# Row maxima of a neighbourhood attention: one head a product over 128 rows, or two heads in two 64-row halves

## The chip, the cores and the metric

One Trainium2 chip, one of its cores. The metric is the device time of one execution of the whole program, in microseconds (us). The engines of a core are TensorE (PE in the profile, its weight loads PEld), VectorE (DVE), ScalarE (ACT), GpSimd (POOL) and SyncE (SP, here only an issuer of DMAs). Each takes its instructions in a fixed order; they wait for each other by semaphores.

## What is computed

Two layers of a diffusion backbone over 2048 latent tokens, 256 context tokens and 1024 channels. Layer 0 mixes latent attention and gated linear attention. Layer 1, which the change is about, is a neighbourhood attention of 16 heads of 64 channels: the tokens lie on a grid of 32 rows by 64 columns, and each query sees the keys in a window of 8 by 16 around it, with a bias from a table, and all 256 context tokens.

```python
def odd_mixer(h, hc, w_in, q_gain, k_gain, rpb, w_out, update_ctx):
    q, k, v, z = ...                       # h @ w_in, split in four; q and k normed per head
    o = neighborhood_attention(q_x, k_x, v_x, k_c, v_c, rpb)
    y = jnp.dot(o.reshape(...) * jax.nn.silu(z_x), w_out)

# in neighborhood_attention, per grid row:
    s_lat = jnp.einsum('bqhd,brkhd->bhqrk', qr, kb) * scale + bias
    s_lat = jnp.where(col_mask, s_lat, -jnp.inf)
    s_ctx = jnp.einsum('bqhd,bchd->bhqc', qr, k_ctx) * scale
    p = jax.nn.softmax(jnp.concatenate([s_lat, s_ctx], axis=-1), axis=-1)
    o = p[..., :kr * GRID_W] @ vb + p[..., kr * GRID_W:] @ v_ctx
```

The softmax needs, for every query and head, a number near the maximum of its scores to subtract before the exponential. The kernel computes these maxima (the "maxima" below) ahead of the attention proper.

## The kernel before

The program runs in stages. Layer 0 comes first, then `odd_qk` projects q and k of layer 1, then `odd_vz` projects v and z and computes the maxima beside it, then `odd_attention` and the output projection follow. The change is in `odd_vz` and in the helper `weave`.

**The projections in `odd_vz`.** There are 18 tiles of 128 tokens (2 of context, 16 latent) and four column blocks of 512, `j` = 4, 5 for v and 6, 7 for z. A cell is one (tile, block); 66 of the 72 are computed here. A cell is 8 steps of `mm3_steps` (L129 to L131), each of three 128-row products into one PSUM bank called "gm", of which there are two. A v cell ends with a copy by ScalarE into `ovz` and two stores on GpSimd's DMA queue (L1201). A z cell ends with a tanh by ScalarE, an operation by VectorE (L1227), four transposes into a bank "tp" (L1230), a copy `ozt` by ScalarE and a store. When a tile is finished, the next one's activations are loaded into `x` and split in `reload` (L357 is its VectorE part).

**The maxima in `maxes`.** The loop runs over 16 heads. Two heads, a pair, share the key tile `mk` (128 rows: 64 channels of either head). Each head loads a bias table `mtab` (L1248, 899 KB) into one of two buffers, and GpSimd adds the row mask and the column mask to it (L1249, L1250). Then come 16 blocks `R` of 128 queries (8 grid rows by 16 columns; `g` is the row group, `c` the column group). Every fourth block, 512 queries are loaded into `mq` (L1258) and copied by ScalarE into the head's own 64 rows of a tile `mz` whose other 64 rows are zero, so that a product over all 128 rows of the array gives the scores of one head. Each block is two products: against the 256 context keys (L1264), two blocks to a bank, and against the window of keys (L1271), 264 to 480 columns, in a bank of its own. VectorE takes the context maxima of two blocks at once (L1266), and then goes through the window in 1 to 4 rectangular pieces, each adding a part of the table and taking the maximum (L1277, an operation and a read of its accumulator). The banks "mx" are five. After the 16 blocks the maxima are reduced (L1282), transposed (L1284), copied by ScalarE (`mr`) and stored in four DMAs on GpSimd's queue (L1288).

**The order.** `weave` alternates two generators: `main` gives the projections' steps, `side` those of the maxima, `ratio` of the second for one of the first. `issue_after(x)` keeps what is made inside it behind the instruction `x`. With a lag of 15, a projection step is only held behind the maxima's step that lies 15 back; within that, a scheduler decides where an instruction stands on its engine. It also decides, for the DMA queues of SP and POOL, in which order the loads and stores are issued. In this stage it spreads the products of the maxima singly between those of the projections.

Of the kernel before, what the change touches and what calls it, by code (L numbers as in the profile page):

```python
# [21 lines left out]
CTX = 256  # L22
T = SEQ + CTX
# [65 lines left out]
class Kern:  # L89
# [1113 lines left out]
    def odd_vz(self, ws, win, hT):  # L1203
        nc = self.nc
        self.z1 = self.scr("z1", (KD, P, SEQ), F32)
        self.M1 = self.scr("M1", (16, SEQ), F32)
        NR, NC = (len(b) for b in BLOCKS["q"])
        with ExitStack() as es:
# [6 lines left out]
            def cell(t, j):  # L1215
# [9 lines left out]
                    return  # L1225
                self.last_tanh = self.act(n[:], ps[:], AF.Tanh, scale=0.5)
                nc.vector.scalar_tensor_tensor(out=n[:], in0=n[:], scalar=1.0, in1=ps[:], op0=ALU.add, op1=ALU.mult)  # L1227
                pt = self.tl(pp, [P, 4, P], "tp", bufs=1)
                for i in range(4):
                    nc.tensor.transpose(pt[:, i, :], n[:, i * P : i * P + P], self.ident[:])  # L1230
                z = self.tl(sp, [P, 4, P], "ozt", bufs=1)
                self.act(z[:], pt[:])
                o = (t - NCT) * P
                nc.scalar.dma_start(self.z1[(j - 6) * 4 : (j - 6) * 4 + 4, :, o : o + P].rearrange("j p t -> p j t"), z[:])

            zq = [[self.tl(mp, [P, 512], f"mz{i}{a}", F32R, bufs=1) for a in range(2)] for i in range(2)]
            for i in range(2):
                for z in zq[i]:
                    nc.vector.memset(z[64 - i * 64 : 128 - i * 64].bitcast(F32), 0.0)

            def maxes():
                for h in range(16):
                    j, b = h // 2, (h % 2) * 64
                    if b == 0:
                        k = self.tl(mp, [P, T], "mk", F32R, bufs=2)
                        nc.sync.dma_start(k[:].bitcast(F32), self.K1[j])
                    tb = self.tl(mp, [P, NR, NC], "mtab", bufs=2)
                    nc.sync.dma_start(tb[:], self.i["rpb_q"][h].rearrange("p (r c) -> p r c", r=NR))  # L1248
                    nc.gpsimd.tensor_tensor(out=tb[:], in0=tb[:], in1=mk[:, :NR].unsqueeze(2).to_broadcast([P, NR, NC]), op=ALU.add)  # L1249
                    nc.gpsimd.tensor_tensor(out=tb[:], in0=tb[:], in1=mk[:, NR:].unsqueeze(1).to_broadcast([P, NR, NC]), op=ALU.add)  # L1250
                    m = self.tl(mp, [P, 16, 5], "mm")
                    nc.vector.memset(m[:], -3e38)
                    kl = k[:, CTX:].rearrange("d (r c) -> d r c", r=32)
                    for R in range(16):
                        g, c = divmod(R, 4)
                        if c == 0:
                            q = self.tl(mp, [P, 512], "mq", F32R, bufs=1)
                            nc.sync.dma_start(q[b : b + 64].bitcast(F32), self.Q1[0, j, b : b + 64, g * 512 : g * 512 + 512])  # L1258
                            zt = zq[h % 2][g % 2]
                            self.by_tile(zt[b : b + 64], q[b : b + 64])  # L1260
                        lh = zt[:, c * P : c * P + P]
                        if c % 2 == 0:
                            pc = self.tl(pp, [P, 2, CTX], "mx", bufs=5)
                        nc.tensor.matmul(pc[:, c % 2, :], lh, k[:, :CTX], start=True, stop=True)  # L1264
                        if c % 2 == 1:
                            nc.vector.tensor_reduce(out=m[:, R - 1 : R + 1, 0], in_=pc[:], axis=AX.X, op=ALU.max)  # L1266
                        (r0, nr), (c0, w) = rect("q", g, c)
                        ps = self.tl(pp, [P, 512], "mx", bufs=5)
                        a, n, d = even(c0, w)
                        ps = ps[:, : nr * n].rearrange("p (r c) -> p r c", r=nr)  # L1270
                        mm = nc.tensor.matmul(ps, lh, kl[:, r0 : r0 + nr, a : a + n], start=True, stop=True)  # L1271
                        ps = ps[:, :, d : d + w]
                        n = 1
                        for ro, ri, rn in pieces("q", 0, g, r0, nr):
                            for co, ci, cn in pieces("q", 1, c, c0, w):
                                s = ps[:, ro : ro + rn, co : co + cn]
                                nc.vector.tensor_tensor_reduce(out=s, in0=s, in1=tb[:, ri : ri + rn, ci : ci + cn], scale=1.0,  # L1277
                                                               scalar=-3e38, op0=ALU.add, op1=ALU.max, accum_out=m[:, R, n : n + 1])
                                n += 1
                        yield mm  # L1280
                    mc = self.tl(mp, [P, 16], "mc", bufs=1)
                    nc.vector.tensor_reduce(out=mc[:], in_=m[:], axis=AX.X, op=ALU.max)  # L1282
                    pt = self.tl(pp, [P, 512], "mx", bufs=5)
                    nc.tensor.transpose(pt[:16, :P], mc[:], self.ident[:])  # L1284
                    r = self.tl(mp, [P, P], "mr", F32R, bufs=1)
                    self.act(r[:16], pt[:16, :P], AF.Copy, scale=-1.0)
                    for g in range(4):
                        nc.gpsimd.dma_start(self.M1[h, g * 512 : g * 512 + 512].rearrange("(a c b) -> c a b", a=8, c=4),  # L1288
                                            r[4 * g : 4 * g + 4].rearrange("c (a b) -> c a b", a=8).bitcast(F32))
# [393 lines left out]
```

## Time and profile before

| | |
|---|---|
| Time, median of 3 runs | 3739.16 us (3738.85 to 3740.12) |
| The profiled execution's own time | 3741.73 us |
| Its span | 3739.6 us |
| `odd_vz` beside the maxima | about 2642 to 3071 us of the span |
| Projections alone after the last product of the maxima | to about 3104 us |
| GpSimd in 2642 to 3071 us | busy 178.1 of 429 us |

The page of the profile gives for each engine its busy time; groups of instructions by line give a count, the busy time, the mean of one, and the idle time ahead of them with what ended it. The busy time of a PE instruction contains pipelining: one projection product shows about 0.39 us while the next begins 0.23 us later. What a product costs the stage is therefore read from the starts of the instructions in the timeline, not from their durations.

### The profile page before, as it was taken

The numbers are of one execution on the slowest core, as the hardware profiler recorded it, in microseconds if no ns is written. First come the engines' busy times: TensorE is split into PE (matmuls) and PEld (weight loads), VectorE is DVE, ScalarE is ACT, GpSimd is POOL, SyncE is SP. The second block draws the span as 40 slices with busy tenths as digits, with TensorE's granted clock in tenths as the row PEclk, the third lists the DMA queues.
The fourth block names the chain that finished last, engine by engine and source line by source line (L and its number), as shares of the span: only waits on it lengthen the run. The fifth ranks groups of instructions, "written<-read, shape, count | busy, mean of one in ns | idle before, by whom it ended". The sixth has DMA issues, their size and how long they took to land.

```text
span 3739.6 us, 51736 instructions
## 1 busy us (share of the span) xinstructions
PE 3583.3 (96%) x18404; PEld 2768.3 (74%) x18404; DVE 2379.7 (64%) x4860; ACT 1437.7 (38%) x2741; POOL 1207.2 (32%) x1334
## 2 busy tenths in 40 slices
PE   8999989999999999999999999999899998898889
PEld 6988988888886666655657878887788885555567
DVE  4677656888866666697654344545678774666722
ACT  4445541111125555545552134444322223454400
POOL 1434330001011222212202233333344435776643
PEclk9999999999999999999999999999999998999899
DMA  7455462222252241434515545546544448777464
GB/s 254 137 165 160 128 172 94 84 75 86 74 137 66 69 114 56 115 88 137 142 51 169 165 148 149 146 142 182 183 141 143 130 116 223 186 182 201 141 194 132
DMA packets 365267, 512.18 MB, mean 137 GB/s; under 512 B 25825, under 2 KB 244913, under 8 KB 359106
## 3 DMA queue, kind: packets, MB, share of 16 engines
q1 hardware_dynamic: 322642, 425.49, 39.7%
q0 software_dynamic: 19712, 55.40, 4.9%
q10 hardware_dynamic: 22656, 27.99, 2.1%
q8 instruction: 146, 2.39, 0.3%
q14 instruction: 111, 0.91, 0.1%
HBM read 329.38 MB, written 179.37 MB: 136 GB/s over the span
## 4 chain that ended last, share of the span: by engine, by line
PE 79%; DVE 7%; DMA 6%; POOL 3%; ACT 3%; issue 2%; SPq 0%; POOLq 0%; DVEq 0%; ACTq 0%
PE gm L129 9%; PE gm L130 9%; PE gm L131 9%; PE av L905 7%; PE st L963 4%; PE mx L651 4%; PE st L964 3%; PE st L965 3%; PE pj L129 3%; PE pj L131 3%; PE pj L130 3%; DMA wraw<-w_od 2%; PE o L1393 2%; PE st L1363 2%; PE o L1375 1%
## 5 line engine op out<-in xcount | busy, mean ns | idle before, releaser
L954 DVE TENSOR_TENSOR acc<-acc,apt 128x512 f32<-128x512 f32 x512 | 364.5, 736 | 156.6 <-ACT apt L106 153.6
L106 ACT ACTIVATE apt<-st 128x512 f32<-128x512 f32 (+1 forms) x592 | 343.9, 593 | 283.9 <-PE st L965 246.5
L652 DVE TENSOR_REDUCE mm<-mx 128x1 f32<-128x512 f32 (+1 forms) x656 | 389.1, 628 | 82.2 <-PE mx L651 75.2
L905 PE MATMUL av<-apt,av 128*64 128x512 f32 (+1 forms) x1184 | 286.2, 597 | 0.0
L963 PE MATMUL st<-aq,akh 97*128 97x512 f32 (+1 forms) x592 | 254.1, 429 | 5.9 <-ACT apt L106 3.0
L1399 POOL TENSOR_TENSOR oacc<-oacc,opt 128x576 f32<-128x576 f32 (+6 forms) x192 | 221.4, 1179 | 86.6 <-ACT opt L106 84.9
L651 PE MATMUL mx<-mk,mq 96*128 96x512 f32 (+1 forms) x656 | 236.8, 373 | 5.8 <-DMA mq<-QT 4.6
L964 PE MATMUL st<-aq,akh 96*128 96x512 f32 (+1 forms) x592 | 235.1, 397 | 0.0
L965 PE MATMUL st<-aq,akl 96*128 96x512 f32 (+1 forms) x592 | 233.9, 396 | 0.0
L1277 DVE CUSTOM_DVE_ANT_1 mx<-mx,mtab 128x225 f32<-128x225 f32 (+13 forms) x576 | 183.6, 339 | 57.8 <-PE mx L1271 42.6
L106 ACT ACTIVATE u<-gm 128x352 f32<-128x352 f32 (+1 forms) x140 | 68.5, 497 | 369.5 <-PE gm L131 208.8
L905 PEld LDWEIGHTS av<-apt,av 128*64 128x64 f32 x1184 | 81.6, 137 | 155.4 <-issue 154.1
L1521 DVE TENSOR_TENSOR opt<-st,tab 128x64 f32<-128x64 f32 (+10 forms) x576 | 142.4, 315 | 79.9 <-PE st L1364 52.7
L963 PEld LDWEIGHTS st<-aq,akh 97*128 97x128 f32 x592 | 112.4, 190 | 99.0 <-issue 43.7
L1073 POOL TENSOR_TENSOR px<-py,px 128x512 f32<-128x512 f32 x64 | 86.3, 1349 | 234.3 <-DVE py L1072 223.0
L106 ACT ACTIVATE opt<-opt 128x930 f32<-128x930 f32 (+8 forms) x130 | 104.4, 805 | 138.9 <-DVE opt L1521 130.1
L1363 PE MATMUL st<-q,kt 128*128 128x480 f32 (+5 forms) x256 | 104.3, 409 | 47.7 <-DVE opt L1521 43.4
L651 PEld LDWEIGHTS mx<-mk,mq 96*128 96x128 f32 x656 | 121.7, 189 | 17.3 <-issue 5.0
L106 ACT ACTIVATE prh<-pr 128x1024 fp32r<-128x1024 f32 x32 | 33.8, 1057 | 261.6 <-PE pj L130 234.0
L965 PEld LDWEIGHTS st<-aq,akl 96*128 96x128 f32 x592 | 113.6, 192 | 25.6
L964 PEld LDWEIGHTS st<-aq,akh 96*128 96x128 f32 x592 | 114.1, 193 | 18.0
L129 PE MATMUL gm<-w1h,hhi 128*128 128x512 f32 x288 | 116.4, 404 | 6.0 <-ACT onat L106 6.0
(511 smaller groups left out, 10033.2 us busy)
## 6 DMA issues: line engine op xcount, KB each, us to landing
q<-Q SPq DMA_DIRECT2D x48, 512.0 KB
H<-x ACTq DMA_DIRECT2D x36, 512.0 KB
adaw<-ada_w SPq DMA_DIRECT2D x64, 256.0 KB
x<-H SPq DMA_DIRECT2D x32, 512.0 KB
pr<-RT SPq DMA_DIRECT2D x32, 512.0 KB
wraw<-w_od SPq DMA_DIRECT2D x64, 256.0 KB
K1t<-okt POOLq DMA_DIRECT2D x32, 512.0 KB, 7.4
kt<-K1t SPq DMA_DIRECT2D x32, 512.0 KB
```

The source lines that it names most:

```text
L106: return self.nc.scalar.activation(out, in_, func, **kw)
L129: self.nc.tensor.matmul(out, lh(k), rh(k), start=j == 0, stop=False)
L130: self.nc.tensor.matmul(out, lh(k), rl(k), start=False, stop=False)
L131: yield self.nc.tensor.matmul(out, ll(k), rh(k), start=False, stop=j == n - 1)
L651: mm = nc.tensor.matmul(ps[:, :w], q[:A_QK, (t % 6) * P : (t % 6) * P + P], k[:A_QK, k0 : k0 + w], start=True, stop=True)
L652: nc.vector.tensor_reduce(out=m[:, t, n : n + 1], in_=ps[:, :w], axis=AX.X, op=ALU.max)
L905: nc.tensor.matmul(O[j, nb][i * 64 : i * 64 + 64, :w], V[j, kt // TT][:, kt % TT, i * 64 : i * 64 + 64], pts[i][:, :w], start=n == 0, stop ...
L954: nc.vector.tensor_tensor(out=acc[i][:, :w], in0=a[:, :w], in1=pts[i][:, :w], op=ALU.add)
L963: nc.tensor.matmul(ps[:, :w], kh[: A_QK + 1, i, kq], qh[: A_QK + 1, :w], start=True, stop=False)
L964: nc.tensor.matmul(ps[:, :w], kh[:A_QK, i, kq], ql[:A_QK, :w], start=False, stop=False)
L965: mm = nc.tensor.matmul(ps[:, :w], kl[:A_QK, i, kq], qh[:A_QK, :w], start=False, stop=True)
L1399: self.psum = nc.gpsimd.tensor_tensor(out=a, in0=a, in1=pts[:, :, a0 - r0 : a1 - r0, :], op=ALU.add)
```

## The change

Inside `maxes` the loop runs over the 8 pairs instead of the 16 heads, and a step is two blocks of both heads: four products against the context keys and four against the windows. Each product takes 64 rows of the array, the lower half for the first head and the upper half for the second, alternating, so `mz` needs no zeros: one copy fills all 128 rows. Each of the six banks of a step is of the kind "mx" (now six); the transposes of z and of the maxima take theirs from the same six, and "tp" is gone. The bias tables of both heads of a pair are held at the same time, in one buffer for each of the two. In `weave`, a lag of zero now also holds each step of the maxima behind the projection step before it, so that the two alternate strictly; the ratio is 0.13 steps of the maxima (eight products) for one of the projections (three products), and the lag is 0.

```diff
@@ weave
-                if next(main, self) is self:
+                step = next(main, self)
+                if step is self:
                     break
...
-                r = next(side, None)
+                with ExitStack() if lag else self.tc.issue_after(step.ins):
+                    r = next(side, None)
@@ odd_vz, cell
-                pt = self.tl(pp, [P, 4, P], "tp", bufs=1)
+                pt = self.tl(pp, [P, 512], "mx", bufs=6)
...
-            zq = [[self.tl(mp, [P, 512], f"mz{i}{a}", F32R, bufs=1) for a in range(2)] for i in range(2)]
-            for i in range(2):
-                for z in zq[i]:
-                    nc.vector.memset(z[64 - i * 64 : 128 - i * 64].bitcast(F32), 0.0)
...
@@ odd_vz, maxes
-                for h in range(16):
-                    j, b = h // 2, (h % 2) * 64
...
-                    tb = self.tl(mp, [P, NR, NC], "mtab", bufs=2)
+                for j in range(8):
+                    k = self.tl(mp, [P, T], "mk", F32R, bufs=2)
+                    nc.sync.dma_start(k[:].bitcast(F32), self.K1[j])
+                    tabs, m = [], []
+                    for i in range(2):
+                        tb = self.tl(mp, [P, NR, NC], f"mtab{i}", bufs=1)
+                        nc.sync.dma_start(tb[:], self.i["rpb_q"][2 * j + i].rearrange("p (r c) -> p r c", r=NR))
+                        nc.gpsimd.tensor_tensor(out=tb[:], in0=tb[:], in1=mk[:, :NR].unsqueeze(2).to_broadcast([P, NR, NC]), op=ALU.add)
+                        nc.gpsimd.tensor_tensor(out=tb[:], in0=tb[:], in1=mk[:, NR:].unsqueeze(1).to_broadcast([P, NR, NC]), op=ALU.add)
+                        tabs.append(tb)
+                        m.append(self.tl(mp, [P, 16, 5], f"mm{i}"))
+                        nc.vector.memset(m[i][:], -3e38)
...
                         if c == 0:
                             q = self.tl(mp, [P, 512], "mq", F32R, bufs=1)
-                            nc.sync.dma_start(q[b : b + 64].bitcast(F32), self.Q1[0, j, b : b + 64, g * 512 : g * 512 + 512])
-                            zt = zq[h % 2][g % 2]
-                            self.by_tile(zt[b : b + 64], q[b : b + 64])
+                            nc.sync.dma_start(q[:].bitcast(F32), self.Q1[0, j, :, g * 512 : g * 512 + 512])
+                            zt = self.tl(mp, [P, 512], "mz", F32R, bufs=2)
+                            self.by_tile(zt[:], q[:])
+                        if c % 2:
+                            continue
+                        bank = lambda: self.tl(pp, [P, 512], "mx", bufs=6)
+                        pc = [bank() for i in range(2)]
+                        for u in range(2):
+                            for i, h in enumerate(half):
+                                nc.tensor.matmul(pc[i][:, u * CTX : u * CTX + CTX], zt[h, (c + u) * P : (c + u) * P + P], k[h, :CTX],
+                                                 start=True, stop=True)
+                        wins = []
+                        for u in range(2):
+                            (r0, nr), (c0, w) = rect("q", g, c + u)
+                            a, n, d = even(c0, w)
+                            for i, h in enumerate(half):
+                                ps = bank()[:, : nr * n].rearrange("p (r c) -> p r c", r=nr)
+                                mm = nc.tensor.matmul(ps, zt[h, (c + u) * P : (c + u) * P + P], kl[h, r0 : r0 + nr, a : a + n],
+                                                      start=True, stop=True)
+                                wins.append((i, u, ps[:, :, d : d + w], (r0, nr), (c0, w)))
+                        for i in range(2):
+                            nc.vector.tensor_reduce(out=m[i][:, R : R + 2, 0], in_=pc[i][:].rearrange("p (u c) -> p u c", u=2),
+                                                    axis=AX.X, op=ALU.max)
+                        for i, u, ps, (r0, nr), (c0, w) in wins:
...
                         yield mm
...
-            self.weave(gemms, maxes(), 0.57, 15)
+            self.weave(gemms, maxes(), 0.13, 0)
```

The end of a pair does what the end of a head did, twice: reduce, transpose, copy, four stores.

More of the change, by code (lines that the diff above doesn't have):

```diff
@@ new lines, in maxes @@
+                for j in range(8):
[10 more added lines that the diff above has]
+                        nc.vector.memset(m[i][:], -3e38)
+                    half = [slice(i * 64, i * 64 + 64) for i in range(2)]
@@ L1265, in maxes @@
[L1265 to L1279, printed above, removed]
@@ new lines, in maxes @@
+                        yield mm
+                    for i in range(2):
+                        mc = self.tl(mp, [P, 16], "mc", bufs=1)
+                        nc.vector.tensor_reduce(out=mc[:], in_=m[i][:], axis=AX.X, op=ALU.max)
+                        pt = self.tl(pp, [P, 512], "mx", bufs=6)
+                        nc.tensor.transpose(pt[:16, :P], mc[:], self.ident[:])
+                        r = self.tl(mp, [P, P], "mr", F32R, bufs=1)
+                        self.act(r[:16], pt[:16, :P], AF.Copy, scale=-1.0)
+                        for g in range(4):
+                            nc.gpsimd.dma_start(self.M1[2 * j + i, g * 512 : g * 512 + 512].rearrange("(a c b) -> c a b", a=8, c=4),
+                                                r[4 * g : 4 * g + 4].rearrange("c (a b) -> c a b", a=8).bitcast(F32))
```

32 lines of the change are left out of this document (9 added, 23 removed).

## The prediction

> **What bounds the kernel now.** I read the page first (span, busy times), then the busy times of the stage that holds the maxima, then who waited for whom in it.
>
> ```profile
> span 3739.6 us, 51736 instructions
> PE 3583.3 (96%) x18404; PEld 2768.3 (74%) x18404; DVE 2379.7 (64%) x4860; ACT 1437.7 (38%) x2741; POOL 1207.2 (32%) x1334
> ...
> 2642.00:3071.00 429.00, 419.88 (x2063) 349.80 (x2062) 332.21 (x1366) 113.77 (x189) 178.10 (x150) 1.00 0.43 134
> ```
>
> The last line is the busy time of PE, PEld, DVE, ACT and POOL in the stretch in which the maxima run: TensorE is busy for 419.9 of 429 us at a full clock, VectorE for 332.2. The stage is a row of products without gaps; whatever stops that row is added to the time.
>
> ```profile
> DVE mx L1277 <- PE mx L1271: 42.6, 81, 1.3
> ...
> SPq L1248 <- DVE mm L1277: 45.9, 14, 5.9
> ...
> POOL mtab L1249 <- DMA mtab<-rpb_q: 25.9, 13, 3.9
> ```
>
> These are waits in the same stretch (total, times, longest). VectorE waits for TensorE, not the other way round. The second and third line are the chain of the bias tables: SP waits until VectorE has used a buffer for the last time, then GpSimd waits for the load. Nobody waits for GpSimd in turn, because with two buffers taken in turn by the heads a table is fetched while the other head, some 26 us of work (16 heads in about 416 us), is computed.
>
> **The products.** The starts of neighbouring products give their slots.
>
> ```profile
> 2701.43 0.40 PE L131 MATMUL gm<-w3h,hlo 128*128 128x512 f32 x1
> 2701.66 0.40 PE L1264 MATMUL mx<-mk,mz 128*128 128x256 f32 x2
> 2701.90 0.39 PE L129 MATMUL gm<-w3h,hhi 128*128 128x512 f32 x1
> ...
> 2702.59 0.38 PE L1271 MATMUL mx<-mk,mz 128*128 128x480 f32 x1
> 2702.80 0.39 PE L129 MATMUL gm<-w3h,hhi 128*128 128x512 f32 x1
> ```
>
> A projection product takes 0.23 us, two context products 0.24 us, a window of 480 columns 0.21 us. By the code a window has 371 columns on average; 0.21 x 371/480 = 0.16 and 0.12 x 371/256 = 0.17, and I take 0.17 us. The 512 products of the maxima cost 256 x (0.12 + 0.17) = 74 us now. In halves of the array their number stays 512, but two go at once if the halves overlap. The trace has such a place in layer 0, where the gated attention alternates products of 64 rows between the halves:
>
> ```profile
> 1306.16 0.40 PE L965 MATMUL st<-aq,akl 96*128 96x512 f32 x1
> 1306.49 1.16 PE L760 MATMUL gl<-gqT,gkT 64*128 64x128 f32 x16
> 1307.58 0.50 PE L963 MATMUL st<-aq,akh 97*128 97x512 f32 x1
> ...
> 2677.12 0.44 PE tp L1230 x4
> ```
>
> Sixteen products of 128 columns are over 1.09 us after they begin. Full-height ones of 128 columns take 0.44 / 4 = 0.11 us (last line), so sixteen would take 1.76 us and eight pairs 0.88 us: the halves do overlap. The rest, 1.09 - 0.88 = 0.21 us, and the entry, 0.33 us from L965 instead of 0.23, are what changing between whole and half array costs: 0.31 us. The changed kernel does that once a step, 64 times: 74 / 2 + 64 x 0.31 = 57 us, a saving of 17 us. Bounds: 37 us saved if the change costs nothing; 20 us lost if halves do not overlap.
>
> **VectorE and the fixed order.** Operations of VectorE stay as many; GpSimd's additions too; ScalarE's copies of queries halve from 64 to 32, off the path.
>
> ```profile
> L1277 DVE CUSTOM_DVE_ANT_1 mx<-mx,mtab 128x225 f32<-128x225 f32 (+13 forms) x576 | 183.6, 339 | 57.8 <-PE mx L1271 42.6 <-PE mx L1264 8.0
> L1250 POOL TENSOR_TENSOR mtab<-mtab,maskq 128x1798 f32<-128x1798 f32 x16 | 60.3, 3774 | 0.8
> L1249 POOL TENSOR_TENSOR mtab<-mtab,maskq 128x1798 f32<-128x1798 f32 x16 | 51.3, 3205 | 31.3 <-DMA mtab<-rpb_q 25.9 <-DVE mm L1277 5.4
> L357 DVE TENSOR_TENSOR hlo<-x,hhi 128x1024 fp32r<-128x1024 f32 x15 | 26.3, 1750 | 4.5 <-ACT hhi L106 4.5
> L1227 DVE SCALAR_TENSOR_TENSOR ovz<-ovz,gm 128x512 f32<-128x512 f32 x30 | 20.4, 679 | 4.5 <-ACT ovz L106 4.5
> ```
>
> A step of the changed kernel is 1 / 0.13 = 7.7 projection steps of three products, 23.1 x 0.23 = 5.3 us, then eight products, 0.58 + 0.31 us, and the transposes of z, 32 x 0.44 / 64 = 0.2 us: a period of 6.4 us. VectorE has 332.2 / 64 = 5.2 us of work in it. A step needs all six banks, which the step before held, so from now on TensorE waits whenever VectorE is a period late. On average it has 1.2 us to spare, but a step that also has L357 (1.75 us) or L1227 (0.68 us) ahead of its last window uses that up, and z's transposes, now in the same banks and a fixed place, wait for L1227. I take 5 us over the stage, between 0 and 20 (0.3 us a step).
>
> **The bias tables.** This is the term that decides. Both tables of a pair are in use until the pair's last step, and each has one buffer. The next pair's loads can only be issued after the last use by VectorE, and nothing of the next pair's windows can be finished until they are loaded and masked. What that chain takes is in the rows of SP and POOL:
>
> ```profile
> 2738.45 0.34 SPq L1248 DMA_DIRECT2D mtab<-rpb_q  x1
> 2739.66 2.33 POOL L1288 DMA_DIRECT2D M<-mr  x4 [11.71 <-ACT mr L106]
> 2743.09 3.21 POOL L1249 TENSOR_TENSOR mtab<-mtab,maskq 128x1798 f32<-128x1798 f32 x1 [1.09 <-DVE mm L1277]
> 2746.25 1.14 POOL L1201 DMA_DIRECT2D V<-ovz  x2
> 2747.41 3.74 POOL L1250 TENSOR_TENSOR mtab<-mtab,maskq 128x1798 f32<-128x1798 f32 x1
> ...
> 2864.57 0.34 SPq L1248 DMA_DIRECT2D mtab<-rpb_q  x1
> ...
> 2873.68 3.21 POOL L1249 TENSOR_TENSOR mtab<-mtab,maskq 128x1798 f32<-128x1798 f32 x1 [3.53 <-DMA mtab<-rpb_q]
> ```
>
> From issue to the first addition are 4.6 us in the one case and 9.1 us in the other. In the changed kernel two such loads are issued together, but the first needs only its own 899 KB; I take 6 us, nearer the short one, which has no other load beside it. On GpSimd the changed program, as built, has this order at every change of pair: four stores of the first head's maxima, L1249's addition for the first table, the same for the second, four stores of the second head's maxima, L1250's addition for the first, then for the second; in four of seven changes two stores of v stand between as well.
>
> Count from the start A of the last step of a pair. VectorE's part in it, 5.2 us less some 0.8 for L357, L1227 and the like ((26.3 + 20.4) / 64 = 0.7), begins 0.3 us later and ends, with one such operation between, at A + 5.0. The first table is ready 0.1 (issue) + 6.0 + 3.2 + 3.2 + 2.3 + 3.7 + 0.3 (small gaps) = 18.8 us after that, A + 23.8. Meanwhile TensorE, in its fixed order, does 24 products of the projections, the first step of the new pair, 24 more, and of the second step what finds a bank: the two context pairs, and two windows in the banks that the context maxima leave. The last two windows need the banks of the first step's windows of the first head. As VectorE's instructions stand, these are free after eight pieces, 8 x 0.32 us (183.6 / 576) = 2.6 us: A + 26.4. The products behind them, the projections, go on at A + 26.7; without the wait it would be 2 x 6.4 + 0.9 = A + 13.7. The stop is 13.0 us, and 0.6 us more on average for the stores of v (4/7 x 1.14). VectorE then does the second head's pieces while 24 projection products pass, so nothing is late next. Bounds for one change: 11.6 us with the short load, 17.2 with the long one and the stores.
>
> A stop of that length has a second price:
>
> ```profile
> 3572.84 0.79 PE L129 MATMUL pj<-wo0h,prh 128*128 128x512 f32 x1 [12.73 <-ACT prh L106]
> ...
> 3572.50:3576.50 4.00, 3.66 (x9) 2.89 (x10) 1.23 (x1) 0.47 (x2) 3.39 (x1) 0.50 1.08 359
> 3579.00:3583.00 4.00, 4.00 (x19) 3.23 (x18) 0.69 (x1) 0.00 (x0) 2.50 (x2) 1.00 0.84 216
> ```
>
> After 12.73 us of idleness the granted clock is 0.50, and TensorE does 9 products in 4 us where it does 19 later. That is (1 - 9/19) x 4 = 2.1 us in this window alone; I take 2.1, so 15.7 us a change and 7 x 15.7 = 110 us. The Trainium skill (TensorE: Matmul & The Clock Gate, Part 1) has the clock at half after an idle window of about 3.4 us and back after one busy window of as long; that would be 1.7 us a stop, by an estimate from its figure, and the sum 3 us less. The row agrees in kind.
>
> **The first pair** has no older table to wait for, but by GpSimd's new order the second table is ready two additions (7 us) after the first, which holds the second and third step: 4 us, between 0 and 8. **The end:** after the last product of the maxima stand 105 projection products instead of 157 (24 us instead of 36), so the loads of the next stage have less to hide behind; I take nothing, between 5 us won (the stores of the maxima out of the way) and 10 lost.
>
> **Sum** against the profiled execution's own 3741.7 us: -17 + 5 + 110 + 4 + 0 = +102, 3844 us. The runs' median is 2.5 us below that execution, so 3841 us.
>
> **The rivals.**
> (1) Faster: the stops at the change of pair are hidden, and only the halves, the banks and the start are left: 3739 - 17 + 5 + 4 = 3731 us. For it: SP, POOL and the load have been off the path so far (no wait for L1250 among the stage's). It decides where table and pieces are through before the second step's last windows are due: A + 13.4 less 5.0 less 2.6 leaves 5.8 us for the chain. Against it: two additions alone take 3.2 + 3.7 = 6.9 us, the shortest load 4.6. For the whole to be faster the stops would have to stay under 8 / 7 = 1.1 us each. 6%.
> (2) The halves do not overlap for these longer products: +20 instead of -17, 3878 us. Against it: the row L760, for it only that there the products have 128 columns. 7%.
> (3) VectorE becomes the bound in every step, not just at times: if its pieces are taken singly behind products that now come in one bunch, the period is what VectorE takes with its waits, say 6.4 + 0.4: 64 x 0.4 = 26 us for my 5, 3862 us. For it: 5.2 of 6.4 us; against it: VectorE's idle time now is spent waiting for TensorE. The Trainium skill says that tiling the array speeds up TensorE but not the emptying of PSUM, which may become the bottleneck (TensorEngine Tiling (Array Packing), Performance Considerations). 17%.
> (4) The stops are shorter and the halves cheaper: the short load (1.4 us less), the stores of both heads out of the way before it lands (2.3 us less), so 15.7 - 3.7 = 12.0 us a change, and 0.1 us instead of 0.31 us for leaving and entering the whole array, which saves 37 - 64 x 0.1 = 31 us: 7 x 12.0 - 31 + 5 + 4 = +62, 3801 us. For it: the load of 4.6 us; against it: GpSimd's new order, and the two rows around L760. 15%.
>
> **How the numbers follow.** My forecast holds 55%. The likeliest is 3841 us. With stops of 11.6 + 2.1 and of 17.2 + 2.1 us (96 to 135 us) its own range is 3827 to 3866 us; widened by the ends for halves, banks and tail and by rivals 3 and 4 the range is 3795 to 3880 us, which leaves out rival 1 and some of rival 2. A measurement of this kernel cannot tell less than about 0.2% (7.5 us) from no change. Faster by more: 0.05; within: 0.02; slower by more: 0.93.
>
> **What would show it.** In the profile after: waits of VectorE's L1277 successor for POOL, and of TensorE's window product for VectorE, seven times each, of 11 to 17 us, with the granted clock at 0.50 after each; slots of two alternating products no longer than one of before (right) or twice that (rival 2); between the stops, TensorE without gaps (right) or waiting for VectorE in most steps (rival 3). I am wrong if the stage has no stop at a change of pair, or if the table lands and is masked within 6 us of its last use.

## The result

| | before | after |
|---|---|---|
| Time, median | 3739.64 us (3738.85 to 3745.35, 4 runs) | 3869.31 us (3867.75 to 3871.41, 4 runs) |
| Ratio, 95% interval | | 1.0339 [1.0326, 1.0352] |
| Span of the profiled execution | 3739.6 us | 3866.0 us |
| First to last product of the maxima | 2655.0 to 3069.4 us | 2659.3 to 3199.4 us |
| Last product of the projections | 3105.9 us | 3224.0 us |
| First product of the attention | 3106.2 us | 3231.5 us |

The change costs 130 us, 3.4%. The profile after has a span 126.4 us longer; first the page, then the busy times of PE, PEld, DVE, ACT and POOL in the stretch of the maxima, then the waits in it (total, times, longest):

```profile
span 3866.0 us, 51638 instructions
PE 3611.2 (93%) x18404; PEld 2754.6 (71%) x18404; DVE 2344.6 (61%) x4856; ACT 1418.2 (37%) x2709; POOL 1201.4 (31%) x1334
...
2642.00:3199.00 557.00, 460.28 (x2114) 345.46 (x2112) 293.54 (x1337) 96.75 (x160) 175.62 (x150) 0.90 0.34 104
...
DVE mm L1279 <- PE mx L1267: 157.6, 65, 6.1
PE mx L1275 <- DVE mm L1286: 60.6, 7, 9.6
DVE mx L1286 <- POOL mtab L1248: 57.9, 15, 8.7
POOL mtab L1247 <- DMA mtab<-rpb_q: 19.3, 7, 8.8
PE mx L1267 <- ACT mz L106: 15.1, 1, 15.1
PE mx L1275 <- DVE mm L1279: 9.2, 21, 0.8
```

TensorE's products are as many as before (18404), but the stretch has 97 us in which it does nothing, and its clock is 0.90 on average instead of 1.00. Seven waits of TensorE for VectorE's pieces make 60.6 of them, and VectorE's wait for GpSimd's second addition to a table stands behind these: one for each change of pair. One more wait, of 15.1 us, is for the first queries. VectorE on the other hand waits 157.6 us for TensorE's context products: it is not the bound between the stops.

One change of pair, from the first pair to the second; A, the start of the last step's products, is 2709.97:

```profile
2714.47 0.81 SPq L1246 DMA_DIRECT2D mtab<-rpb_q  x2
2717.19 2.34 POOL L1298 DMA_DIRECT2D M<-mr  x4 [2.87 <-ACT mr L106]
2721.89 6.37 POOL L1247 TENSOR_TENSOR mtab<-mtab,maskq 128x1798 f32<-128x1798 f32 x2 [2.36 <-DVE ovz L1229]
2728.21 2.28 POOL L1298 DMA_DIRECT2D M<-mr  x4
2730.51 7.28 POOL L1248 TENSOR_TENSOR mtab<-mtab,maskq 128x1798 f32<-128x1798 f32 x2
2734.21 0.20 DVE L1286 CUSTOM_DVE_ANT_1 mx<-mx,mtab 128x32 f32<-128x32 f32 x1 [7.71 <-POOL mtab L1248]
2735.53 0.99 PE L1275 MATMUL mx<-mk,mz 64*128 64x264 f32 x2 [8.55 <-DVE mm L1286]
2736.45 0.79 PE L129 MATMUL gm<-w3h,hhi 128*128 128x512 f32 x1
```

The loads go out at A + 4.5, the two additions to both tables and the stores between them follow one after the other, and the first piece starts at A + 24.2. TensorE ran out of banks at A + 17.0, waits 8.55 us for two banks, and goes on with the projections at A + 26.5, at first at half speed: the first product shows 0.79 us instead of 0.39.

The two places where time was lost but none was expected to speak of, the start and the end:

```profile
2646.82 0.53 SPq L1258 DMA_DIRECT2D mq<-Q  x1
2658.61 0.63 ACT L106 ACTIVATE mz<-mq 128x512 fp32r<-128x512 f32 x1 [2.50 <-DMA mq<-Q]
2659.29 0.79 PE L1267 MATMUL mx<-mk,mz 64*128 64x256 f32 x4 [15.12 <-ACT mz L106]
...
3202.85 1.79 SPq L111 DMA_DIRECT2D q<-Q  x3
3231.53 0.76 PE L1373 MATMUL st<-q,kc 128*128 128x512 f32 x1 [7.16 <-DMA q<-Q]
```

The first queries are issued behind the first key tile and both tables, and are copied 11.8 us later; the fixed order lets no projection product past the first product of the maxima meanwhile. At the end the attention's queries are issued 28.7 us before the attention begins. In the kernel before it was 36.8 us:

```profile
3069.38 1.97 SPq L111 DMA_DIRECT2D q<-Q  x3
```

### The profile page after: what moved, and what is told of

The parts are those of the page before. It is cut to its first block, busy times and chain, and to the rows that moved or that the text cites. A ratio compares the mean times of both kernels' runs of the same rounds, so it can differ in the third digit from the quotient of the medians.

```text
span 3866.0 us, 51638 instructions
## 1 busy us (share of the span) xinstructions
PE 3611.2 (93%) x18404; PEld 2754.6 (71%) x18404; DVE 2344.6 (61%) x4856; ACT 1418.2 (37%) x2709; POOL 1201.4 (31%) x1334
## 4 chain that ended last, share of the span: by engine, by line
PE 76%; DMA 8%; DVE 6%; POOL 5%; ACT 2%; issue 2%; SPq 0%; POOLq 0%; DVEq 0%; ACTq 0%
PE gm L129 9%; PE gm L130 9%; PE gm L131 8%; PE av L907 7%; PE st L965 4%; PE mx L653 4%; PE st L966 3%; PE st L967 3%; PE pj L129 3%; PE pj L130 3%; PE pj L131 3%; PE o L1403 2%; PE st L1373 1%; DMA wraw<-w_od 1%; DVE oacc L1393 1%
## 5 line engine op out<-in xcount | busy, mean ns | idle before, releaser
L1286 DVE CUSTOM_DVE_ANT_1 mx<-mx,mtab 128x465 f32<-128x465 f32 (+16 forms) x576 | 167.9, 360 | 58.9 <-POOL mtab L1248 57.9
L1279 DVE TENSOR_REDUCE mm<-mx 128x2 f32<-128x512 f32 x128 | 82.8, 688 | 157.6 <-PE mx L1267 157.6
L1203 POOL DMA_DIRECT2D V<-ovz x60 | 32.1, 539 | 328.8 <-ACT ovz L106 328.8
```

## The experiments

The kernel before took between 3732.7 and 3741.1 us beside them. Where one time is given, it is one run with its profile; a difference of less than some 8 us between such runs says nothing by itself; where it is used, it is by the waits in the traces.

**Tables loaded once.**

```diff
-                    tabs, m = [], []
+                    if j == 0:
+                        tabs = []
+                    m = []
                     for i in range(2):
-                        tb = self.tl(mp, [P, NR, NC], f"mtab{i}", bufs=1)
+                        if j == 0:
+                            tb = self.tl(mp, [P, NR, NC], f"mtab{i}", bufs=1)
...
```

> The changed kernel, but the bias tables are loaded and masked for the first pair only and used by all eight (the other fourteen tables are left out, so the maxima of later heads carry the wrong bias). Theory (the chain last use, load, four additions, stores between, holds TensorE at each of the seven changes of pair): in the changed kernel the second step of a pair takes 20.4 us instead of 6.9, seven times, 95 us; without the chain these steps fall to about 7 us and the time to about 3775 us. Rival (the strict order alone, or VectorE as the bound, makes these stops): the second steps stay above 10 us and the time above 3840 us.

3781.28 us, span 3779.5: 86.5 us less than the changed kernel, and not one wait of TensorE for the pieces of the maxima (L1289 here) is left. The longest waits of TensorE that remain are these (the window products are on L1278 here, the context products on L1270):

```profile
PE mx L1270 <- ACT mz L106: 15.2, 1, 15.2
PE st L1376 <- DMA q<-Q: 7.2, 1, 7.2
PE mx L1232 <- DVE ovz L1229: 6.1, 5, 2.2
PE mx L1278 <- DVE mm L1282: 4.7, 10, 0.6
```

So the tables make two thirds of the loss; some 40 us are something else, 22 of them the first two of these lines. The same kernel, run four more times (below), took 3774.53 us; by that the tables make 95 of the 130 us.

**One mask addition instead of two.** Row and column mask are added once into a tile of their own; a table then needs one addition.

```diff
+            mk2 = self.tl(mp, [P, NR, NC], "maskq2", bufs=1)
+            nc.gpsimd.memset(mk2[:], 0.0)
+            nc.gpsimd.tensor_tensor(out=mk2[:], in0=mk2[:], in1=mk[:, :NR].unsqueeze(2).to_broadcast([P, NR, NC]), op=ALU.add)
+            nc.gpsimd.tensor_tensor(out=mk2[:], in0=mk2[:], in1=mk[:, NR:].unsqueeze(1).to_broadcast([P, NR, NC]), op=ALU.add)
...
-                        nc.gpsimd.tensor_tensor(out=tb[:], in0=tb[:], in1=mk[:, :NR].unsqueeze(2).to_broadcast([P, NR, NC]), op=ALU.add)
-                        nc.gpsimd.tensor_tensor(out=tb[:], in0=tb[:], in1=mk[:, NR:].unsqueeze(1).to_broadcast([P, NR, NC]), op=ALU.add)
+                        nc.gpsimd.tensor_tensor(out=tb[:], in0=tb[:], in1=mk2[:], op=ALU.add)
-                n = self.tl(sp, [P, 512], "ovz", bufs=3)
+                n = self.tl(sp, [P, 512], "ovz", bufs=2)
-                            zt = self.tl(mp, [P, 512], "mz", F32R, bufs=2)
+                            zt = self.tl(mp, [P, 512], "mz", F32R, bufs=1)
```

> The two masks are added once into a tile of their own, so a table needs one addition instead of two (for the room, three ovz buffers become two and two mz buffers one). My theory: the first table is ready 9 us sooner, some 15.1 us after the start of the last step instead of 24.2; TensorE ran out of banks at 17.0 us in the changed kernel, so the stops of 7.7 to 8.7 us vanish but for some 1 us, and the clock stays full: 3780 to 3800 us, nearest 3785, beside 3781 with tables loaded once. Rival: the stop is set by the load and by VectorE's arrears rather than by GpSimd's additions: 3825 us or more.

3806.89 us, span 3805.1: 60.9 us less. The long stops are gone, as the theory says: TensorE's seven waits for pieces are now 4.6 us in all, and VectorE hardly waits for a table.

```profile
PE mx L1279 <- DVE mm L1283: 10.0, 22, 0.8
PE mx L1279 <- DVE mm L1290: 4.6, 7, 0.7
PE mx L1271 <- ACT mr L106: 4.5, 4, 2.5
DVE mx L1290 <- POOL mtab L1252: 1.9, 3, 1.5
```

It missed the expected 3785 by 22 us nevertheless. Behind a change of pair there is a handful of short waits instead, and the clock falls all the same. The windows at the change from the second to the third pair (the last three columns are granted clock, DMA share, GB/s):

```profile
2776.00:2779.00 3.00, 3.00 (x14) 2.46 (x14) 0.23 (x1) 0.60 (x1) 2.23 (x1) 1.00 0.86 338
2779.00:2782.00 3.00, 2.41 (x13) 1.66 (x12) 0.78 (x2) 0.74 (x2) 3.00 (x2) 1.00 0.02 5
2782.00:2785.00 3.00, 1.80 (x6) 0.91 (x4) 3.00 (x20) 0.00 (x0) 3.00 (x2) 0.78 0.29 87
2785.00:2788.00 3.00, 3.00 (x8) 2.19 (x9) 2.90 (x27) 0.63 (x1) 2.01 (x4) 0.50 0.27 58
2788.00:2791.00 3.00, 3.00 (x10) 2.35 (x9) 0.71 (x8) 0.00 (x0) 0.00 (x0) 0.58 0.10 33
```

VectorE is busy without a pause from 2782 to 2788 with the pieces it is behind, TensorE is held four times for 0.3 to 0.6 us, and then works at 0.50: 8 and 10 products in 3 us instead of 14. The number of additions decides whether there is a long stop; being late by a step still costs (3807 - 3781) / 7 = 3.7 us a change, or 4.6 us beside the 3774.5 us. This version also gives up one `ovz` and one `mz` buffer for the room, and no run separates that.

**Stores of the maxima on SP's queue.**

```diff
-                            nc.gpsimd.dma_start(self.M1[2 * j + i, g * 512 : g * 512 + 512].rearrange("(a c b) -> c a b", a=8, c=4),
+                            nc.sync.dma_start(self.M1[2 * j + i, g * 512 : g * 512 + 512].rearrange("(a c b) -> c a b", a=8, c=4),
```

> The four stores of the maxima go to SP's queue instead of GpSimd's. My theory: the chain of the tables sets the stop, and the second head's stores (2.28 us) stand in it between GpSimd's additions, so that each of the seven stops is some 2.3 us shorter: 3869 - 16 = 3853 us, first piece of a new pair 21.9 us after the start of the last step instead of 24.2. Rival: the stores only use time in which GpSimd waits for a table anyway, or SP holds the queries behind them: 3865 us or more.

3861.37 us, span 3859.6: 6.4 us less, between theory and rival. That is too little for one run to show; the profile separates two parts that are larger:

```profile
PE mx L1275 <- DVE mm L1286: 44.2, 7, 7.5
DVE mx L1286 <- POOL mtab L1248: 41.4, 15, 6.6
PE st L1373 <- DMA q<-Q: 18.5, 1, 18.5
...
3183.38 5.87 SPq L1298 DMA_DIRECT2D M<-mr  x8
3189.41 1.79 SPq L111 DMA_DIRECT2D q<-Q  x3
```

The seven stops are 44.2 instead of 60.6 us, 2.3 us less each, as the four stores between GpSimd's additions take (2.28 us). The first piece after the change shown above starts 22.0 us after A. But the last pair's eight stores now stand 5.9 us long ahead of the attention's queries on SP, and the wait for these is 18.5 instead of 7.2 us: 16.4 us won, 11.3 us given back.

**A later start.**

```diff
-            self.weave(gemms, maxes(), 0.13, 0)
+            self.weave(gemms, maxes(), 0.135, 0, 9)
```

> The changed kernel with the maxima begun nine projection steps later (27 products, 6.2 us) and at 0.135 instead of 0.13 a step. Theory (the first product of the maxima waits 15.1 us for the first queries, which land at a fixed moment behind tables and weights, and the fixed order puts it there): about 6 us of the 15 are filled with projections, and the step that follows loses its half clock only in part: 3858 us, the first stop about 9 us. Rival (the stop only moves behind, to the second step that waits for the second table): 3866 us.

3858.02 us, span 3856.2: the number is the theory's, and the first stop is shorter by 6.5 us. But the sum is in part luck: the seven stops at a change of pair became 8.2 us shorter too (52.4 instead of 60.6 us), which the theory did not have, and not all of it reached the total.

```profile
2658.77 0.58 PE L1267 MATMUL mx<-mk,mz 64*128 64x256 f32 x2 [8.59 <-ACT mz L106]
```

**Full height in the fixed order, twice.** The same steps, banks and order, but every product over 128 rows with the zero-padded `mz` of the kernel before: once with the tables as in the changed kernel, once with tables for the first pair only. Beside the latter stands the kernel with tables loaded once, in halves, run four more times.

```diff
+            zq = [[self.tl(mp, [P, 512], f"mz{i}{a}", F32R, bufs=1) for a in range(2)] for i in range(2)]
...
-                                nc.tensor.matmul(pc[i][:, u * CTX : u * CTX + CTX], zt[h, (c + u) * P : (c + u) * P + P], k[h, :CTX],
+                                nc.tensor.matmul(pc[i][:, u * CTX : u * CTX + CTX], zt[i][:, (c + u) * P : (c + u) * P + P], k[:, :CTX],
...
-                                mm = nc.tensor.matmul(ps, zt[h, (c + u) * P : (c + u) * P + P], kl[h, r0 : r0 + nr, a : a + n],
+                                mm = nc.tensor.matmul(ps, zt[i][:, (c + u) * P : (c + u) * P + P], kl[:, r0 : r0 + nr, a : a + n],
```

> The changed kernel with the products over all 128 rows again, on queries padded with zeros as before, in the same fixed order, steps, banks and tables; ScalarE copies the queries of the two heads apart. Theory by the trace of the changed kernel (a step of eight products takes 0.59 us in halves plus 0.41 us for leaving and entering the whole array, against 1.16 us): 64 x 0.16 = 10 us more outside the stops, 3870 to 3880 us. By the prediction's term of 17 us: 3883 us. Rival (halves do not overlap): 3850 us or less.

> Tables for the first pair only, with zero-padded products over the full height of the array in the same fixed order, so that the halves are priced without the stops: against 3781 us of the same kernel in halves. My theory: eight full products take 1.16 us and never change the array, eight in halves 1.03 us with the change: 64 x 0.13 = 8 us more, 3789 us. The prediction's term (17 us): 3798 us. Rival: no gain in halves at all: 3782 us or less.

> The kernel with tables for the first pair only once more, with rounds, because the zero-padded version of it came out at 3773 us and not above its 3781 us, which was one run. My theory: by the slots of undisturbed steps (1.02 us in halves, 1.25 us padded in the same order) the halves are worth 64 x 0.23 = 15 us, of which the waits for VectorE take back most: 3765 to 3773 us, the first run having been a slow one. Rival: the halves bring nothing or cost something in the whole: 3777 us or more.

With the tables' stops: 3870.98 us, 3.2 us more in span than in halves, which one run cannot tell from nothing. Without them: 3772.65 us at full height (3769.26 to 3775.43), 3774.53 us in halves (3769.28 to 3776.92; the first run of it, 3781.28, lies above all of these), between the last theory's 3773 and its rival's 3777 us. So in the whole the halves bring nothing that can be measured in this order, and the theory that expected 8 us more at full height missed. In the slots they do bring something. A step of the changed kernel that nothing disturbs:

```profile
2757.71 0.40 PE L131 MATMUL gm<-w2h,hlo 128*128 128x512 f32 x1
2758.03 0.50 PE L1267 MATMUL mx<-mk,mz 64*128 64x256 f32 x4
2758.37 0.55 PE L1275 MATMUL mx<-mk,mz 64*128 64x360 f32 x4
2758.86 0.50 PE L129 MATMUL gm<-w2h,hhi 128*128 128x512 f32 x1
2759.19 0.39 PE L130 MATMUL gm<-w2l,hhi 128*128 128x512 f32 x1
```

From L131 to L130 are 1.48 us; less two slots of 0.23, the eight products cost 1.02 us with entering and leaving the halves. That is also the median of the 21 such steps with nothing beside them. At full height in the same order it is 1.25 us (25 steps): 64 x 0.23 = 15 us, if all steps were like these.

Nearly half are not. Some 30 of the 64 steps stand right behind z's four transposes, which now take one of the same six banks. The step's last window needs that bank again, and its weight load (PEld) waits until ScalarE has copied the transposes out of it. The first line is from the waits of the changed kernel, the second is one of the 27 places:

```profile
PEld mx L1275 <- ACT ozt L106: 6.3, 27, 0.3
...
2690.00 0.18 PEld L1275 LDWEIGHTS mx<-mk,mz 64*128 64x128 f32 x1 [0.23 <-ACT ozt L106]
```

There the transposes and the eight products take 1.76 us together in halves and 1.69 us at full height, whose trace has no such wait (medians of 20 undisturbed places in each of the two kernels without table stops). So the halves win 0.23 us in one kind of step and lose 0.07 us in the other. From the first product of the maxima to the attention the two kernels take 480.6 us (halves) and 478.5 us (full). By the starts in the trace, some 10 of the 15 us are lost among the maxima's own products, most of it at this bank; 3 us go to a longer wait for the queries at the end (7.4 instead of 4.5 us), and 2 to 4 us to the clock at half, which lasts for more projection products in halves.

**Twice as many changes of the array.** Context products and windows as steps of their own, 64 more entries into the halves.

```diff
+                        for i in range(2):
+                            nc.vector.tensor_reduce(out=m[i][:, R : R + 2, 0], in_=pc[i][:].rearrange("p (u c) -> p u c", u=2),
+                                                    axis=AX.X, op=ALU.max)
+                        yield mm
                         wins = []
...
-            self.weave(gemms, maxes(), 0.13, 0)
+            self.weave(gemms, maxes(), 0.26, 0)
```

> A step of the maxima is cut in two: the four context products in one place, the four window products 3.85 projection steps later; TensorE goes into the halves 128 times instead of 64. My theory: a change costs 0.41 us a round trip as the starts in the trace give it, so 64 more cost 26 us where nothing else changes; VectorE's work is spread better, which can give back some of the 13 us of small waits: 3880 to 3897 us, nearest 3888. Rival: a change of half costs 0.2 us or less: 3869 to 3880 us, or less with the better spread.

3894.58 us, span 3892.8: 26.8 us more, 0.42 us an entry. The slots agree: context steps take 0.64 and window steps 0.78 us (medians of 33 and 46 undisturbed ones), together 1.42 instead of 1.02 us, 0.40 us for the second round trip. The slots are the better measure, for the whole contains other changes both ways: z's transposes wait 21.3 us for VectorE instead of 5.9, the seven stops are 56.1 instead of 60.6 us, and the waits for context maxima 3.9 instead of 9.2.

**A looser order.**

```diff
-            self.weave(gemms, maxes(), 0.13, 0)
+            self.weave(gemms, maxes(), 0.13, 2)
```

> The changed kernel with a lag of 2 steps instead of 0: the projections are held only behind the step of the maxima two back, and the maxima are no longer held behind the projections; halves, banks, tables and GpSimd's work as they are. Theory (the chain of tables is a delay that projections can fill if the order lets them pass): up to two steps of projections, 46 x 0.23 = 10.6 us, stand between the last product that needs no table and the first that does, so the seven stops of 8.7 us mostly go, and so does the first of 15 us: 3770 to 3800 us. Rival (the banks or the weight of the chain itself are the limit, whatever the order): above 3840 us.

3902.07 us, span 3900.3: the theory missed, in sign too. It had only the stops in view, and these did shrink:

```profile
PE mx L1275 <- DVE mm L1286: 22.4, 13, 5.5
PE mx L1275 <- DVE mm L1279: 17.7, 21, 4.2
PE st L1373 <- DMA q<-Q: 14.5, 1, 14.5
PE mx L1267 <- ACT mz L106: 4.9, 1, 4.9
```

But with a lag the scheduler takes the eight products apart again: counted in the trace, TensorE goes into the halves 198 times instead of 64. 134 more at 0.40 us are 54 us; against them stand 30 us less of waiting for VectorE and 10 us at the start, and 7 us more at the end. That makes 21 of the 34 us. Of the rest, some 11 us are the clock: 140 projection products instead of 83 start 0.43 us apart and not 0.23.

**What is left without any of the stops, and versions of the whole.** Three kernels start later. The first has the tables loaded once, the second one mask addition a table, both with this edit:

```diff
-            self.weave(gemms, maxes(), 0.13, 0)
+            self.weave(gemms, maxes(), 0.135, 0, 22)
```

> Tables loaded and masked for the first pair only (the others use these), and the maxima start 22 projection steps later at 0.135 steps for one, so that neither the tables nor the first query holds anything. What is then left of the change are the halves, the six banks and the fixed order. My theory: the first stop of 15 us goes, the small waits stay, so 3781 - 14 = 3767 us, that is some 25 to 30 us above the kernel before. Rival: the halves win once nothing waits for tables: 3745 us or less.

> One mask addition a table, and the maxima start 22 projection steps later at 0.135 steps for one; all that the reference wants is computed. My theory: 3807 less the first stop of 14 us, 3793 us, of which some 4 us a change of pair are left as short waits and half clock. Rival: with a step 0.25 us shorter VectorE falls behind as in the version with 0.14, and it is 3805 us or more; or the later start also takes the short waits away and it comes near the kernel before, 3750 us or less.

The third has one mask addition, the stores of the maxima on SP's queue, and

```diff
-            self.weave(gemms, maxes(), 0.13, 0)
+            self.weave(gemms, maxes(), 0.14, 0, 22)
```

> One mask addition a table, stores of the maxima on SP's queue, the maxima start 22 projection steps later and go at 0.14 steps for one. My theory: the stops at a change of pair (95 us), the first stop (17 us) and the wait for the queries after the stage (7 us) are gone, and what is left beside the kernel before are the halves (8 us won) and small waits for VectorE (13 us or more, since a step is 0.4 us shorter): 3745 to 3770 us, nearest 3755, not below the kernel before. Rival: VectorE, at 5.2 of about 6.2 us a step, becomes the bound and waits appear in most steps: 3780 us or more; or the halves are worth more than 8 us, and it comes out under 3739 us.

Tables loaded once: 3767.04 us (3761.79 to 3780.61), ratio to the kernel before 1.0084 [1.0062, 1.0105]. The number is the one expected, but not shown to be so for the reason expected: in the profiled run, the slowest of the four, the first stop is still there, as a wait of z's transposes for VectorE (below, with the hardware), and the other three runs have no trace. One mask addition: 3804.43 us (3799.35 to 3808.10), 1.0176 [1.0159, 1.0193]; the later start took 2 us, where 14 were expected. The first stop of 13.8 us is gone there, but z's transposes wait 16.3 us for VectorE instead of 6.2. With 0.14 steps and SP's queue: 3813.11 us, the rival's number: VectorE waits for tables again (17.2 us), z's transposes for VectorE (16.2 us), and the attention for its queries (10.3 us). No version of the halves in a fixed order came below the kernel before, not even the one that loads a table only once.

## Why the prediction held, and where its sum was off

3841 us was forecast, 3869 measured, inside the range and on the right side, by the mechanism that was to decide. The sum was +102; the spans differ by +126.4:

| Term | Predicted | Measured |
|---|---|---|
| Products in halves | -17 | -11, by slots of undisturbed steps |
| VectorE and the fixed order | +5 | about +17, as the rest |
| Seven changes of pair, with the clock | +110 | +94 |
| First pair | +4 | +17 |
| The end | 0 | +7 |
| Start of the stage, after the stage | not in it | +2.5 |

**The tables' chain** was right step by step: A + 5.0 predicted and 4.5 measured for the last use, A + 23.8 and 24.2 for the first piece, A + 26.7 and 26.5 for the projections. From issue to the first addition were 7.4 us here, and 5.9 to 7.5 us at the seven changes, where 6 were taken, and the end of the last step came 0.5 us sooner. The step that failed is the subtraction: "without the wait it would be 2 x 6.4 + 0.9 = A + 13.7". A step takes 7.0 us (the median), not 6.4, and the two of this place 7.2 and 7.5; so the second step's banks are asked for at A + 17.0 rather than 13.7, and the chain overlaps with more products. The seven steps with a stop took 142.9 us in all; less 7 x 7.0, that is 94 us, 13.4 a change instead of 15.7. The medians of the changed kernel and of the one with tables loaded once lie as far apart, 94.8 us. The experiments with tables loaded once, one addition, and stores elsewhere each changed one link, and the stop went or shrank with the link: this cause is shown.

**The clock** behind a stop was predicted at 2.1 us. In the changed kernel it is 2.1 us in the mean of the seven stops (1.4 to 2.7): seven to fourteen projection products lose 0.2 us each. The 1.7 us that the prediction estimated from the figure of the Trainium skill (TensorE: Matmul & The Clock Gate, Part 1) lies inside that range, so these stops do not decide between the two.

**The halves** overlap (the two products of a pair start 5 ns apart in the median): rival 2 is out. The step that failed is the size of "changing between whole and half array": 0.40 us, by the doubled changes, where 0.31 was taken from the row L760; the eight products of before cost 2 x 0.24 + 4 x 0.18 = 1.20 us, so that 64 x (1.20 - 1.02) = 11 us would be saved if nothing disturbed a step. Behind z's transposes the eight take 1.76 - 0.44 = 1.32 us, more than before; the table has this loss in its second row.

**The first pair** is the step that failed in kind. It was argued that the second table comes late; what comes late is the first query, which TensorE cannot go round in a fixed order: 15.1 us and the clock. The prediction looked at what the order on GpSimd does to the tables and not at what strict alternation does to the first wait of all. That a start nine steps later shortened this stop from 15.1 to 8.6 us shows it.

**The end** was put at nothing, between 5 won and 10 lost, and the mechanism named (24 us of products instead of 36 cover the next stage's loads) is the one that lost 7.2 us.

**VectorE and the fixed order**: predicted 5, up to 20. The waits of TensorE besides the stops are 20.5 us (9.2 for context maxima, 5.9 for z, 3.1 and 2.3 at the ends of pairs) against 8.9 us before. But 9.4 of them lie in the seven steps with a stop, which the +94 holds already, so waits explain only some 2 of the 17 us. About 8 more are the bank of z's transposes, 27 x 0.30 us beyond a step of 1.02. The prediction had the transposes wait for VectorE in their new place; it did not have the maxima wait for ScalarE's copy of them, since it counted six banks for a step and none for the transposes between two steps. The remaining 7 us are not separated.

Rival 3 is out as a bound in every step: VectorE waits 157.6 us for the products. Rival 1 is out, seven stops. Rival 4's stop of 12.0 us lay nearer the measured 13.4 than the forecast's 15.7 did, but not for its reason: the chain was no shorter (A + 24.2), only the second step came later; and changing the array cost more than 0.31, not 0.1.

## What to carry to other kernels

When two working sets that were fetched in turn are held together in one buffer each, the whole chain from last use over load and preparation to first use moves onto the path: add it up from the rows, and subtract the work that the fixed order really lets pass meanwhile, counted in banks. Strict alternation of two streams makes each wait of the one a stop of both, the very first load too, and each of the seven stops here cost the clock again. Tiling the array pays only by product time less the change: here eight products of 1.2 us gained 0.2 us in a step that nothing disturbed, and waits took that back. Count the banks of everything that draws from a pool: a step that needs all six of them waits for whatever took one in between.

## What the hardware showed that was not expected

**The clock falls after short waits too.** With one mask addition, TensorE's waits at the change from the second to the third pair were 0.59, 0.30, 0.53 and 0.34 us within 4 us, and the clock went to 0.50 (windows above). At another place of the same kernel a single wait of 1.49 us left it at full speed; in the kernel with tables loaded once, one of 1.49 us was followed by seven slow products. The Trainium skill (TensorE: Matmul & The Clock Gate, Part 1) has a window of about 3.4 us that runs freely, which fits that one and the same wait can count or not; its table asks for a whole idle window, but its passage on a second failure mode, in the same part, has short idle times between groups of products do the same in another kernel, as these rows do.

**An operation of VectorE stood behind GpSimd's additions.** The first stop of the kernel without table reloads and with the later start:

```profile
2653.43 6.37 POOL L1250 TENSOR_TENSOR mtab<-mtab,maskq 128x1798 f32<-128x1798 f32 x2
2654.51 13.05 DVE L385 TENSOR_TENSOR w3l<-wraw,w3h 128x512 fp32r<-128x512 f32 x1 [2.18 <-ACT w3h L106]
2659.76 7.25 POOL L1251 TENSOR_TENSOR mtab<-mtab,maskq 128x1798 f32<-128x1798 f32 x2
2667.49 0.68 DVE L1229 SCALAR_TENSOR_TENSOR ovz<-ovz,gm 128x512 f32<-128x512 f32 x1
2668.22 1.11 PE L1232 MATMUL mx<-ident,ovz 128*128 128x128 f32 x4 [11.65 <-DVE ovz L1229]
```

A subtraction that takes 0.69 us in the median took 13.05 us: it ended 0.55 us after the last of GpSimd's four additions, and TensorE's transposes waited 11.65 us behind it. The Trainium skill (SBUF — State Buffer, SBUF: two separate sides) says that VectorE and GpSimd share one pair of ports as a lock, held for a whole instruction, which an operation of VectorE with two inputs in SBUF needs. The row agrees. In it VectorE did not get through between GpSimd's additions either; in the changed kernel it did, where the same kind of subtraction took 2.58 us and ended 0.54 us after the first of the four additions. The kernel before has the same: of the sixteen subtractions on L357 the three that began during an addition of GpSimd took 3.0 to 4.4 us, the others 1.22 us. The pieces of the maxima, with one input in PSUM, ran beside the additions at their usual 0.2 to 0.5 us. No run here took GpSimd's additions away from this place alone, so the cause is argued from the rows and not shown by an experiment.
